# Two attentions of a tuned Trainium2 kernel: scores ahead of the transposes, a division moved, q and k in one bank, one value block moved

## The chip, the cores and the metric

The kernel runs on one core of one Trainium2 chip. The metric is the device time of one execution in microseconds (us), as a median over runs.

A core has five engines that run side by side. Each works through its own instructions strictly in order and waits for others by semaphores. TensorE (PE) does matrix products and transposes into PSUM; its weight loads are listed apart (PEld). VectorE (DVE), ScalarE (ACT) and GpSimd (POOL) do the element work. SyncE (SP) issues the transfers from DRAM.

## The reference, cut to what matters

```python
def layer(i, x):                                   # DEPTH = 2, D = 1024, SEQ = 256, BATCH = 1
    x = post_norm(x, 0.5 * swiglu(x, ffn1_w_in[i], ffn1_w_out[i]))
    x = post_norm(x, fox(x) if i == 0 else mla(x))
    x = post_norm(x, 0.5 * swiglu(x, ffn2_w_in[i], ffn2_w_out[i]))
    return post_norm(x, sigmoid(x @ wg[i] + bg[i]) * (p[i] @ wp[i]))

def fox(x):                                        # layer 0: 16 heads of 64
    q, k, v, f = split(x @ w_in)                   # f: one gate logit per head and token
    cum = cumsum(log_sigmoid(f + b_f), axis=tokens)
    s = q @ k.T / 8 + cum[:, None] - cum[None, :]  # per head, 256 x 256
    return (softmax(causal(s)) @ v) @ w_o

def mla(x):                                        # layer 1: 16 heads, 128 + 64 wide, v 128 wide
    c_q = rms_norm(x @ w_dq)
    q_nope, q_rope = split(c_q @ w_uq); q_rope = rope(q_rope)
    s = (q_nope @ k_nope.T + q_rope @ k_rope.T) / sqrt(192)
    return (softmax(causal(s)) @ v) @ w_o          # k_nope, v from a shared latent c_kv
```

Both attentions sweep blocks of 128 queries. With 256 tokens that is two blocks: the first sees 128 keys, the second 256, so a head's scores fill 128 + 256 = 384 columns of 128 partitions.

## The kernel before

**Precision and weights.** A product in float32 is made of three products of exact parts, high with high, high with low and low with high (`mm3`, whose matmuls are recorded at L418). The parts of a result are made by `parts`: ACT copies the high part (L427), DVE subtracts it to leave the low part (L428). The weights go the same way. A `Stream` knows the order in which weights are used, fetches them into three raw tiles through SP's queue, and splits each unit of up to 1024 columns into a pair: a copy on ACT (L138, about 1.06 us) and a subtraction on DVE (L139, about 1.22 us). Split units wait in ten slots, and in rooms (`ota`, `otb`, `qk`, `fs`) that a stage lends when it doesn't use them. When to split is decided while the program is written: `pump` is called after every `mm3` and issues a split where the next raw tile should have landed and rough clocks of the engines (`busy`, `pair`) say that it holds up nothing. `use` splits at once what is needed now. So moving a step also moves the splits between the steps, on ACT and on DVE.

**What orders the work.** Every engine runs its instructions in the order in which the code issues them. Small steps that should lie between others stand in a queue `bg`: each `use` takes one item off it, and a FoX projection (`ws`) takes one more at its weight blocks 3 and 6. PSUM has three rings of banks of 128 x 512: four `y`, two `h`, two `tr`. Whoever takes a bank waits until its last user but that many is done with it.

**FoX** (function `fox`). The value blocks `V(n, t)` (half n of the columns, tokens t) are projected first: V(0,0), V(1,0), the gates, V(0,1), V(1,1), each into an h bank and then into parts (tag `g`). `gates` puts a chain of eleven items into `bg`: log-sigmoid and running sum of the gate logits on ACT, DVE and POOL (the last of POOL's is L759; ACT's L763 and L764, DVE's L767, L770 and L774 make from it `negc`, the rows that the score product adds). `flush` forces what is left of them, and `gates_transpose` makes `cq`, the per-query terms. Then pairs of heads j = 0 to 7 follow. The steps of a pair:

- `gen_k(j)`, `gen_q(j)`: projections of 24 matmuls each, each into its own h bank and its own parts.
- `QK(j)`: the scores of both heads, two matmuls with `negc` and twelve with q and k.
- `softmax(j)`: four mask steps with a running minimum on DVE (L838), a bias from `cq` (two small operations for each head, L845 and L846), four exponentials on ACT (L850), one reciprocal on DVE (L855), four multiplications by it on POOL (L859). The result is P.
- `T(j)`: six transposes of P into two tr banks (four are recorded at L870, two at L422) and parts PT.
- `AV(j)`: products with the values, into `ota` or `otb`, whose low parts are DVE's L899.
- `O(k, t)`: the output projection of rows k for tokens t.

The loop's order is gen_k(j+1), T(j-1), QK(j), softmax(j), gen_q(j+1), AV(j-1). At j = 7 the projections' places are taken by O(0,0), O(1,0) and O(2,0), O(3,0).

**MLA** (function `mla`). The same steps for one head at a time: `gen(h)` makes k and q in one h bank with one `parts` of 512 columns, `QK(h)` writes into a tr bank, `softmax` has two segments (DVE's mask L1137, ACT's exponentials L1141, reciprocal L1146, POOL's scaling L1148), `T(h)` three transposes, `AV(h)` into an h bank. The order is gen(h+1), T(h-1), QK(h), softmax(h), O(h-2) for both token blocks or, from head `LATE` = 6 on, for the first alone, then a value block V in four of the heads (table `VT`: heads 0, 5, 8 and 10), AV(h-1). The second token block of the late heads follows at the end, partly ahead of the last steps as cover.

Of the kernel before, what the change touches and what calls it, by code (L numbers as in the profile page):

```python
# [13 lines left out]
ALU = mybir.AluOpType  # L14
# [16 lines left out]
LATE = 6  # L31
# [20 lines left out]
class Dummy:  # L52
    """Stands in for engines, pools and tiles while the order of the weights is recorded."""

# [24 lines left out]
class Stream:  # L79
    """Weights in the order of their use: DRAM -> raw tile -> exact pair of float32r parts."""  # L80

# [65 lines left out]
    def lend(self, *tags):  # L147
        """Room that a stage doesn't use."""
        self.retire()
        for t in tags:  # L150
            self.kept.discard(t)
            self.slots.append(t)
# [18 lines left out]
    def busy(self, act=0, dve=0, pe=0):  # L171
        """Keeps rough clocks of the engines, in ns, by the columns that they work on."""
        if act:
            self.act_t = max(self.act_t, self.pe_t) + 200 + 0.84 * act
        if dve:
            self.dve_t = max(self.dve_t, self.pe_t) + 80 + 1.05 * dve
        if pe:
            self.pe_t += max(108, 0.42 * pe)

    def pair(self, n):  # L180
        """The high parts on ScalarE, the low parts on VectorE after them."""
        self.busy(act=n)
        self.dve_t = max(self.dve_t, self.act_t + 100)
        self.busy(dve=n)

    def pump(self):
        """Splits weights ahead of their use where that holds up nothing else."""
        if self.ready == len(self.order) or not self.slots:
            return
        arrival = self.arrives.get(group_of(self.order[self.ready]), 1e12)  # L190
        if arrival <= self.pe_t + 500 and max(self.act_t, self.dve_t) <= self.pe_t + SLACK_NS:
            self.split()
# [29 lines left out]
def unit_of(key, raw):  # L222
    """The part of a raw tile that holds a unit, its partitions and its columns."""
    k, u = key[0], key[-1] % 2
    if k in ("win", "fv"):
        return raw.rearrange("p (k c) -> p k c", c=512)[:, 2 * u : 2 * u + 2, :], 128, 1024
    if k in ("wout", "fo", "pg", "pp", "mo", "qr"):
        return raw[:, 1024 * u : 1024 * u + 1024], 128, 1024
    if k in ("fk", "fq"):
        return raw.rearrange("p (k c) -> p k c", c=256)[:, :, 128 * u : 128 * u + 128], 128, 1024  # L230
    if k == "ff":
        return raw[:, 0:1024], 128, 1024
    if k == "pb":
        return raw[0:1, 0:1024], 1, 1024
    if k == "kd":
        return raw[:, 640 * u : 640 * u + 640], 128, 640
    if k == "dq":
        return raw[:, 768 * u : 768 * u + 768], 128, 768
    if k == "qn":
        return raw[:, 512:1280], 128, 768  # L240
    if k == "kvv":
        return raw[:, 0:1024], 128, 1024
    if k == "kvk":
        return raw[:, 0:512], 128, 512
    raise KeyError(key)
# [83 lines left out]
def pbcast(row, n):  # L329
    """A row of DRAM, read by all partitions."""  # L330
    return bass.AP(tensor=row.tensor, offset=row.offset, ap=[[0, 128], [1, n]])


class Trunk:
# [10 lines left out]
    def own(self, shape, dt, tag):  # L345
        """A tile in room that the weights have given back."""
        self.S.check(tag)
        return self.tl(shape, dt, tag, 1)
# [47 lines left out]
    def spin(self, n):  # L396
        """Keeps the tensor engine's clock up while the first data arrive."""
        hot = self.bank("y")
        for _ in range(n):
            self.nc.tensor.matmul(hot[:, 0:384], self.mask[:, 0:128], self.mask, start=True, stop=True)  # L400
# [7 lines left out]

# [1 line left out]
    def mm3(self, out, lhsT, rhs, start, stop):  # L410
# [14 lines left out]
    def parts(self, hi, lo, src):  # L425
        """src = hi + lo exactly."""
        self.nc.scalar.activation(hi, src, AF.Copy)  # L427
        self.nc.vector.tensor_tensor(lo, src, hi.bitcast(F32), op=ALU.subtract)  # L428
        self.S.pair(cols(src))

    def transposed(self, t, src):
        """Token-major [128, 1024] into xT."""
        for h in range(2):
# [13 lines left out]
    def moving(self, ps, t, name, width, at=None, what=None, sweeps=0):  # L447
        """ps[tokens, width] = x[t] W, the weights moving in units of two k-tiles.

        In sweeps, products of high parts come first, and some low parts come last.  # L450
        """
        order = [(u, terms) for terms in SWEEPS[sweeps] for u in range(4)]
# [22 lines left out]
    def ln_stats(self, st, t, c0, w, y, alpha):  # L475
        """x[t] = alpha x[t] + y in some columns, with their statistics."""
        nc = self.nc
        xs = self.x[t][:, c0 : c0 + w]
        nc.vector.scalar_tensor_tensor(xs, xs, alpha, y, op0=ALU.mult, op1=ALU.add)  # L479
        nc.vector.bn_stats(st, xs)  # L480
        self.S.busy(dve=2 * w)
# [23 lines left out]

# [1 line left out]
    def ffn(self, li, which, lni, kv=False, at=None, cold=False):  # L507
# [81 lines left out]

# [1 line left out]
    def ple_load(self, li):  # L591
# [99 lines left out]

# [1 line left out]
    def fox(self, li):  # L693
# [97 lines left out]
        V(0, 1)  # L791
        V(1, 1)

# [3 lines left out]

        def gen(j, key, c0):
            ps = self.bank("h")
            ws((key, j), ps[:, 0:256])  # L800
            o = qk[:, j % 2]
            self.parts(o[:, 0, c0 : c0 + 256], o[:, 1, c0 : c0 + 256], ps[:, 0:256])

        def gen_k(j):
            gen(j, "fk", 256)

        def gen_q(j):
            gen(j, "fq", 0)

# [19 lines left out]
        def softmax(j):  # L829
# [6 lines left out]
            for s in range(2):  # L836
                for q, (c0, c1) in enumerate(seg):
# [4 lines left out]
                    )  # L842
                c2 = cq[:, 2 * j + s, :]
                i = slice(2 * s, 2 * s + 2)
                nc.vector.tensor_tensor(tt[:, i], nm[:, i], c2, op=ALU.subtract)  # L845
                nc.vector.tensor_tensor(tt[:, i], tt[:, i], c2, op=ALU.add)  # L846
            for s in range(2):
# [6 lines left out]
            self.S.busy(act=1800, dve=1400)  # L854
            nc.vector.reciprocal(su, su)  # L855
            for s in range(2):
                for q, (c0, c1) in enumerate(seg):
                    i = 2 * s + q
                    nc.gpsimd.tensor_scalar(  # L859
                        P[s][:, c0:c1], P[s][:, c0:c1], su[:, i : i + 1], 1.0, op0=ALU.mult, op1=ALU.mult  # L860
                    )
            st[j] = P

        def T(j):
# [42 lines left out]
        def O(k, t):  # L907
# [3 lines left out]
            for n in range(2):  # L911
# [3 lines left out]
                )  # L915

        for j in range(8):
            if j == 2:
# [6 lines left out]
            if j == 0:  # L925
                self.flush()
                gates_transpose()
                S.lend("fs")
            if j >= 1:
                T(j - 1)  # L930
            QK(j, "y" if j < 7 else "h")
            softmax(j)
            if j < 7:
                gen_q(j + 1)
            else:
                O(2, 0)
                O(3, 0)
            if j >= 1:
# [17 lines left out]

# [1 line left out]
    def kv_setup(self):  # L958
# [62 lines left out]

# [1 line left out]
    def mla(self, li):  # L1023
# [106 lines left out]
        def softmax(h):  # L1130
# [14 lines left out]
            self.S.busy(act=900, dve=600)  # L1145
            nc.vector.reciprocal(su[:, 0:2], su[:, 0:2])  # L1146
            for q, (c0, c1) in enumerate(seg):
                nc.gpsimd.tensor_scalar(  # L1148
                    P[:, c0:c1], P[:, c0:c1], su[:, q : q + 1], 1.0, op0=ALU.mult, op1=ALU.mult
                )  # L1150
            st[h] = P

        def T(h):
# [59 lines left out]
        for h in range(16):  # L1213
            if 1 <= h < 15:
                gen(h + 1)
            if h == 15:
                S.lend("qk")
                O(LATE, (1,))
            if h >= 1:
                T(h - 1)  # L1220
            QK(h)
            softmax(h)
            if h >= 2:
                O(h - 2, (0, 1) if h - 2 < LATE else (0,))
            if h == 15:
                O(LATE + 1, (1,))
            if h in VT:
                V(*VT[h], "tr")
            if h >= 1:
                AV(h - 1)  # L1230
        self.load_gb(li, 1)
        O(LATE + 2, (1,))
        O(14, (0,))
        T(15)
        AV(15)
        O(LATE + 3, (1,))
        O(15, (0,))
        self.ln(0, y[0], ALPHA, LN_EPS)
        for h in range(LATE + 4, 16):
            if h == 15:  # L1240
                self.XT(0)
            O(h, (1,))
# [82 lines left out]
```

## Time and profile before

| what | us | share of the span |
|---|---|---|
| median of 3 runs (1127.40, 1127.43, 1129.90) | 1127.43 | |
| span of the profiled execution | 1125.3 | |
| PE busy | 1100.2 | 98% |
| PE weight loads | 922.2 | 82% |
| DVE busy | 715.0 | 64% |
| ACT busy | 543.1 | 48% |
| POOL busy | 79.9 | 7% |

By stage, the windows of the trace give (busy us of each engine in the stretch):

| stretch, us | what runs | length | PE | DVE | ACT | POOL |
|---|---|---|---|---|---|---|
| 0 to 218.8 | first FFN, FoX's V(0,0), V(1,0), gates, V(0,1) | 218.8 | 215.10 | 127.99 | 103.47 | 8.83 |
| 218.8 to 324.8 | FoX, from V(1,1) to AV(7) | 106.0 | 100.34 | 80.93 | 62.76 | 26.18 |
| 324.8 to 768.3 | rest of layer 0, shared keys and values, FFN and MLA's projections | 443.5 | 441.60 | 277.36 | 205.63 | 24.30 |
| 768.3 to 897.7 | MLA's heads | 129.4 | 123.49 | 90.55 | 74.29 | 15.93 |
| 897.7 to 1125.3 | rest of MLA, FFN, end | 227.6 | 219.63 | 138.17 | 97.00 | 4.67 |

How to read rows of the timeline: start, duration, engine, line, operation, output <- input by the program's names, shape, and how many instructions the row groups; in square brackets the idle time before it on that engine and the instruction that ended it. The page gives the profiled execution no time beside its span; the span begins with the first and ends with the last instruction that the profile shows, and the runs' times are 2.1 us longer at the shortest.

### The profile page before, as it was taken

To read this page: it belongs to the slowest core of one execution; us is meant where nothing else is said; L and a number is where in the kernel's file an instruction comes from. 1 tells how busy PE (TensorE), PEld (TensorE's weight loads), DVE (VectorE), ACT (ScalarE), POOL (GpSimd) and SP (SyncE) were. 2 spreads that over 40 slices of the span, in tenths; PEclk is the share of its full clock that TensorE was granted. 3 is DMA by queue.
4 is the path that set the end of the run, shared out by engine and by line. 5 is a ranking of instruction groups with operands and counts; after the bars stand their busy time and mean duration, and the time that the engine had idled before them with its cause. 6 is when DMAs were issued, how large, how long until landed. Compare 5 with 4: busy or idle time off the path is not lost. (4 is left out here: it accounts for less than half of the span.)

```text
span 1125.3 us, 14519 instructions
## 1 busy us (share of the span) xinstructions
PE 1100.2 (98%) x5582; PEld 922.2 (82%) x5582; DVE 715.0 (64%) x1030; ACT 543.1 (48%) x822; POOL 79.9 (7%) x130
## 2 busy tenths in 40 slices
PE   8999999989999999999999999999999999999997
PEld 6888888889878888888888888887899788888886
DVE  5655636777786644557966444488766775554576
ACT  5544533656635544543555444345655454454421
POOL 0000000322210000000320000011111000000000
PEclk9999999989999999999999999999999999999999
DMA  9777644454337765544477665334543566755402
GB/s 298 220 264 249 202 150 131 151 187 151 113 113 225 243 219 183 186 162 148 151 233 243 211 219 166 92 96 140 178 123 113 171 222 221 255 192 182 161 27 75
DMA packets 150537, 198.81 MB, mean 177 GB/s; under 512 B 11714, under 2 KB 128450, under 8 KB 150468
## 3 DMA queue, kind: packets, MB, share of 16 engines
q1 hardware_dynamic: 150468, 197.88, 54.7%
q8 instruction: 44, 0.72, 0.3%
q14 instruction: 25, 0.20, 0.1%
HBM read 196.81 MB, written 1.05 MB: 176 GB/s over the span
## 5 line engine op out<-in xcount | busy, mean ns | idle before, releaser
L139 DVE TENSOR_TENSOR hl<-raw,hl 128x1024 fp32r<-128x1024 f32 (+3 forms) x293 | 345.7, 1197 | 114.9 <-ACT hl L138 109.0
L418 PE MATMUL h<-hl,xT 128*128 128x512 f32 (+1 forms) x1716 | 413.4, 392 | 2.5 <-DVE hl L139 1.5
L418 PEld LDWEIGHTS h<-hl,xT 128*128 128x128 f32 x1716 | 317.4, 188 | 70.4 <-DVE hl L139 2.5
L138 ACT ACTIVATE hl<-raw 128x1024 fp32r<-128x1024 f32 (+3 forms) x293 | 296.0, 1031 | 99.1 <-PE y L418 60.8
L418 PE MATMUL y<-hl,g 128*128 128x512 f32 x792 | 187.1, 391 | 0.0
L418 PEld LDWEIGHTS y<-hl,g 128*128 128x128 f32 x792 | 148.1, 188 | 31.0
L517 ACT ACTIVATE P<-h 128x256 f32<-128x256 f32 x88 | 34.0, 386 | 235.8 <-PE h L418 235.8
L518 DVE TENSOR_TENSOR P<-P,h 128x256 f32<-128x256 f32 x88 | 36.9, 419 | 161.9 <-ACT P L517 161.9
L490 POOL TENSOR_TENSOR rs<-ve,mhalf 128x1 f32<-128x1 f32 x16 | 15.2, 950 | 843.6 <-DVE ve L489 843.6
L427 ACT ACTIVATE xT<-tr 128x512 fp32r<-128x512 f32 x36 | 20.1, 596 | 62.3 <-PE tr L422 62.3
L428 DVE TENSOR_TENSOR g<-tr,g 128x512 fp32r<-128x512 f32 x50 | 34.5, 691 | 24.1 <-ACT g L427 24.0
L418 PE MATMUL h<-xT,hl 128*128 128x256 f32 x360 | 46.8, 289 | 1.8 <-DVE g L428 1.8
L418 PEld LDWEIGHTS h<-xT,hl 128*128 128x128 f32 x360 | 44.8, 197 | 3.1 <-DVE g L428 2.0
L418 PE MATMUL y<-hl,xT 128*128 128x512 f32 (+2 forms) x228 | 44.4, 347 | 0.0
L418 PE MATMUL h<-qk,xT 128*128 128x512 f32 x168 | 43.9, 394 | 0.0
L427 ACT ACTIVATE g<-tr 128x512 fp32r<-128x512 f32 x50 | 29.9, 598 | 24.5 <-PE tr L526 18.6
L418 PEld LDWEIGHTS y<-hl,xT 128*128 128x128 f32 x228 | 37.1, 188 | 5.6 <-issue 0.7
L418 PE MATMUL h<-otb,xT 128*128 128x512 f32 x144 | 37.3, 393 | 0.0
L418 PEld LDWEIGHTS h<-qk,xT 128*128 128x128 f32 x168 | 31.3, 188 | 6.6
L418 PE MATMUL y<-hl,ota 128*128 128x512 f32 x144 | 36.0, 393 | 0.0
L138 ACT ACTIVATE otb<-raw 128x1024 fp32r<-128x1024 f32 x21 | 22.2, 1056 | 20.3 <-PE y L418 14.7
L139 DVE TENSOR_TENSOR qk<-raw,qk 128x1024 fp32r<-128x1024 f32 x21 | 25.8, 1227 | 9.1 <-ACT qk L138 8.8
(204 smaller groups left out, 1289.3 us busy)
## 6 DMA issues: line engine op xcount, KB each, us to landing
raw<-in_ffn_w_in_dram SPq DMA_DIRECT2D x172, 512.0 KB, 5.0
raw<-in_ffn_w_out_dram SPq DMA_DIRECT2D x44, 1024.0 KB, 5.1
raw<-in_fox_w_in_dram SPq DMA_DIRECT2D x12, 1024.0 KB, 5.3
raw<-in_ple_w_gate_dram SPq DMA_DIRECT2D x8, 1024.0 KB, 6.8
raw<-in_mla_w_o_dram SPq DMA_DIRECT2D x8, 1024.0 KB, 6.0
gb<-in_ln_g_dram SPq DMA_DIRECT2D x8, 512.0 KB, 6.9
gb<-in_ln_b_dram SPq DMA_DIRECT2D x8, 512.0 KB, 7.5
raw<-in_fox_w_o_dram SPq DMA_DIRECT2D x4, 1024.0 KB, 5.1
```

The source lines that it names most:

```text
L138: nc.scalar.activation(hi, src, AF.Copy)
L139: nc.vector.tensor_tensor(lo, src, hi.bitcast(F32), op=ALU.subtract)
L418: self.nc.tensor.matmul(out, lhsT, rhs, start=start, stop=stop)
L427: self.nc.scalar.activation(hi, src, AF.Copy)
L428: self.nc.vector.tensor_tensor(lo, src, hi.bitcast(F32), op=ALU.subtract)
L490: nc.gpsimd.tensor_tensor(rs, ve, self.mhalf, op=ALU.pow)
L517: nc.scalar.activation(gt[:, 0:256], ps[:, 0:256], AF.Silu)
L518: nc.vector.tensor_tensor(gt[:, 0:256], gt[:, 0:256], ps[:, 256:512], op=ALU.mult)
```

## The change

Besides docstrings and comments, which are taken out, the change has these parts.

In FoX: (1) V(1,1) is issued inside pair 0, after its softmax and before its division, and no longer ahead of the first key projection. (2) `gen_k` and `gen_q` write into the two halves of one h bank, and one `parts` of 512 columns follows the q projection. (3) The bias is worked out for both heads at once, two operations of 128 x 4 behind all four mask steps. (4) The reciprocal and POOL's scaling become a function `normalize`, which is called after V(1,1) for pair 0, put into the queue `bg` behind one empty item for pairs 1 to 6, and called after O(2,0) for pair 7. (5) QK(j) is issued ahead of T(j-1).

In MLA: QK(h) is issued ahead of T(h-1), the division after the output projection O(h-2), AV(h-1) ahead of the value block V; in head 15 the room `qk` is lent after QK(15), as QK now stands behind O(6, second block). At the end the late second-block projections move one place forward: one stands between T(15) and AV(15), another between AV(15) and O(15, first block).

```diff
-        V(1, 1)
...
-        def gen(j, key, c0):
-            ps = self.bank("h")
-            ws((key, j), ps[:, 0:256])
-            o = qk[:, j % 2]
-            self.parts(o[:, 0, c0 : c0 + 256], o[:, 1, c0 : c0 + 256], ps[:, 0:256])
-        def gen_k(j):
-            gen(j, "fk", 256)
-        def gen_q(j):
-            gen(j, "fq", 0)
+        gen = {}
+        def gen_k(j):
+            gen[j] = self.bank("h")
+            ws(("fk", j), gen[j][:, 256:512])
+        def gen_q(j):
+            ps = gen.pop(j)
+            ws(("fq", j), ps[:, 0:256])
+            o = qk[:, j % 2]
+            self.parts(o[:, 0, :], o[:, 1, :], ps)
...
-                c2 = cq[:, 2 * j + s, :]
-                i = slice(2 * s, 2 * s + 2)
-                nc.vector.tensor_tensor(tt[:, i], nm[:, i], c2, op=ALU.subtract)
-                nc.vector.tensor_tensor(tt[:, i], tt[:, i], c2, op=ALU.add)
+            c2 = cq[:, 2 * j : 2 * j + 2, :].rearrange("p h t -> p (h t)")
+            nc.vector.tensor_tensor(tt, nm, c2, op=ALU.subtract)
+            nc.vector.tensor_tensor(tt, tt, c2, op=ALU.add)
...
+            def normalize():
+                nc.vector.reciprocal(su, su)
+                for s in range(2):
+                    for q, (c0, c1) in enumerate(seg):
+                        i = 2 * s + q
+                        nc.gpsimd.tensor_scalar(
+                            P[s][:, c0:c1], P[s][:, c0:c1], su[:, i : i + 1], 1.0, op0=ALU.mult, op1=ALU.mult
+                        )
...
+        rest = lambda: None
...
+            QK(j, "y" if j < 7 else "h")
             if j >= 1:
                 T(j - 1)
-            QK(j, "y" if j < 7 else "h")
-            softmax(j)
-            if j < 7:
+            normalize = softmax(j)
+            if j == 0:
+                V(1, 1)
+                normalize()
+                gen_q(j + 1)
+            elif j < 7:
+                self.bg.extend((rest, normalize))
                 gen_q(j + 1)
             else:
                 O(2, 0)
+                normalize()
                 O(3, 0)
...
             if h == 15:
+                O(LATE, (1,))
+            QK(h)
+            if h == 15:
                 S.lend("qk")
-                O(LATE, (1,))
             if h >= 1:
                 T(h - 1)
-            QK(h)
-            softmax(h)
+            normalize = softmax(h)
             if h >= 2:
                 O(h - 2, (0, 1) if h - 2 < LATE else (0,))
+            normalize()
             if h == 15:
                 O(LATE + 1, (1,))
+            if h >= 1:
+                AV(h - 1)
             if h in VT:
                 V(*VT[h], "tr")
-            if h >= 1:
-                AV(h - 1)
...
         T(15)
+        O(LATE + 3, (1,))
         AV(15)
-        O(LATE + 3, (1,))
+        O(LATE + 4, (1,))
         O(15, (0,))
         self.ln(0, y[0], ALPHA, LN_EPS)
-        for h in range(LATE + 4, 16):
+        for h in range(LATE + 5, 16):
```

More of the change, by code (lines that the diff above doesn't have):

```diff
@@ L854, in softmax @@
             self.S.busy(act=1800, dve=1400)
[L855 to L861, printed above, removed]
+            def normalize():
[6 more added lines that the diff above has]
+                        )
             st[j] = P
+            return normalize
         def T(j):
@@ L1145, in softmax, with normalize @@
             self.S.busy(act=900, dve=600)
[L1146 to L1150, printed above, removed]
+            def normalize():
+                nc.vector.reciprocal(su[:, 0:2], su[:, 0:2])
+                for q, (c0, c1) in enumerate(seg):
+                    nc.gpsimd.tensor_scalar(
+                        P[:, c0:c1], P[:, c0:c1], su[:, q : q + 1], 1.0, op0=ALU.mult, op1=ALU.mult
+                    )
             st[h] = P
+            return normalize
         def T(h):
```

## The prediction

> **What bounds the kernel now.** I read the page, then the windows by stage, TensorE's timeline through both attentions, and there the queues of VectorE (DVE), ScalarE (ACT) and GpSimd (POOL).
>
> ```profile
> span 1125.3 us, 14519 instructions
> ...
> 218.80:324.80 106.00, 100.34 (x709) 89.18 (x708) 80.93 (x196) 62.76 (x145) 26.18 (x38) 0.97 0.46 146
> ...
> 768.30:897.70 129.40, 123.49 (x818) 110.16 (x817) 90.55 (x191) 74.29 (x160) 15.93 (x34) 1.00 0.44 136
> ```
>
> Columns of a window: length, busy time of PE, weight loads, DVE, ACT, POOL, then granted clock. These are FoX and MLA; PE idles 5.7 and 5.9 us in them. All that the change touches lies here, so it acts only through what PE waits for.
>
> ```profile
> 224.31 2.91 PE L418 MATMUL h<-xT,hl 128*128 128x256 f32 x24
> 229.00 5.90 PE L418 MATMUL h<-xT,hl 128*128 128x256 f32 x48 [1.79 <-DVE g L428]
> 235.05 0.44 PE L418 MATMUL y<-negc,sel 64*128 64x384 f32 x2
> ...
> 244.22 0.78 PE L870 MATMUL tr<-ident,P 128*128 128x128 f32 x2 [2.03 <-POOL P L859]
> 247.21 5.11 PE L418 MATMUL h<-xT,hl 128*128 128x256 f32 x24
> ...
> 264.59 0.60 PE L870 MATMUL tr<-ident,P 128*128 128x128 f32 x4
> ...
> 273.13 0.38 PE L870 MATMUL tr<-ident,P 128*128 128x128 f32 x2
> ```
>
> PE needs 8.54 us for a pair of heads (264.59 to 273.13: two projections of 2.85 us, QK, T, AV). What sets the pace of the later pairs is DVE, which runs this round (pair 3):
>
> ```profile
> 267.70 0.29 DVE L838 CUSTOM_DVE_ANT_0 y<-y,mask 128x128 f32<-128x128 f32 x1
> ...
> 268.80 0.16 DVE L846 TENSOR_TENSOR tt<-tt,cq 128x2 f32<-128x2 f32 x1
> ...
> 269.98 0.16 DVE L846 TENSOR_TENSOR tt<-tt,cq 128x2 f32<-128x2 f32 x1
> 271.26 0.18 DVE L855 RECIPROCAL su<-su 128x4 f32<-128x4 f32 x1 [1.11 <-ACT P L850]
> 272.13 1.29 DVE L139 TENSOR_TENSOR hl<-raw,hl 128x1024 fp32r<-128x1024 f32 x1 [0.70 <-ACT hl L138]
> 273.35 0.41 DVE L428 TENSOR_TENSOR qk<-h,qk 128x256 fp32r<-128x256 f32 x1
> 273.69 0.84 DVE L899 TENSOR_TENSOR ota<-y,ota 64x256 fp32r<-64x256 f32 x2
> 274.56 1.23 DVE L139 TENSOR_TENSOR hl<-raw,hl 128x1024 fp32r<-128x1024 f32 x1
> ...
> 276.16 1.01 DVE L428 TENSOR_TENSOR PT<-tr,PT 128x512 fp32r<-128x512 f32 x2
> 277.09 0.29 DVE L838 CUSTOM_DVE_ANT_0 y<-y,mask 128x128 f32<-128x128 f32 x1
> ```
>
> Mask step to mask step is 9.39 us: 3.56 to the reciprocal, 0.87 to the weight split, 4.96 back to back. DVE idles only where it waits for ACT (1.11 and 0.70). PE's waits for P are what is left over when 9.39 meets 8.54, so covering PE's wait does not shorten the round.
>
> **FoX, the steady round.** Per pair the bias arithmetic goes from four small DVE operations to two (0.2 us each saved), but now stands behind all four mask steps, and all four exponentials of ACT stand behind it.
>
> ```profile
> 269.08 0.37 ACT L850 ACTIVATE P<-y,tt 128x128 f32<-128x128 f32 x1 [2.92 <-DVE tt L846]
> ```
>
> ```profile
> 237.57 1.28 ACT L850 ACT_TABLE_LOAD   x1 [2.24 <-DVE tt L846]
> 238.86 0.37 ACT L850 ACTIVATE P<-y,tt 128x128 f32<-128x128 f32 x1
> ```
>
> ```profile
> 240.62 0.18 DVE L855 RECIPROCAL su<-su 128x4 f32<-128x4 f32 x1 [1.95 <-ACT P L850]
> ```
>
> Before, the first head's exponentials start 1.38 us into the round, under the second head's mask steps. After: both heads' mask steps 1.8, two bias operations 0.36, 0.12 to ACT: start at 2.29; four in a row take 1.76 (238.86 to 240.62); reciprocal at 4.05 instead of 3.56. The "deferred" division does not leave its place: in the built order of pairs 1 to 7 the reciprocal follows the bias operations directly, no split in between. The joined q and k parts are one 128x512 subtraction (0.67 to the next, as PT's first) for two of 0.34: nothing. So 4.05 + 0.87 + 4.96 = 9.88, 0.49 more per pair. QK ahead of T adds PE work of nothing and removes the wait for P; in its place QK's products with the low part of k wait for that joined subtraction, which is queued behind exponentials and a split: 4.05 + 0.87 + 1.22 + 0.69 = 6.83 us into the round. T and PT follow in 0.5 + 1.3 us, just ahead of DVE's own queue (8.9), so 9.88 stands. Pair 1 has three splits in its round instead of two: 11.1.
>
> **FoX, the start.** V(1,1) (24 matmuls, 5.5 us from 218.8 to 224.31; one ACT copy, one DVE subtraction; no DMA, its weights being split for V(0,1)) leaves the place where it covered the gate chain.
>
> ```profile
> 225.84 1.44 POOL L759 TENSOR_SCALAR fs<-fs 32x256 f32<-32x256 f32 x1 [1.08 <-DVE fs L758]
> ```
>
> ```profile
> 227.31 0.30 ACT L763 ACTIVATE negc<-fs 32x128 fp32r<-32x128 f32 x1 [2.21 <-POOL fs L759]
> 227.53 0.40 ACT L764 ACTIVATE negc<-fs 32x256 fp32r<-32x256 f32 x1
> ```
>
> ```profile
> 228.98 0.42 DVE L767 TENSOR_TENSOR negc<-fs,negc 32x256 fp32r<-32x256 f32 x1
> ...
> 230.94 0.35 DVE L774 CAST negc<-negc 64x384 fp32r<-64x384 f32 x1
> ```
>
> POOL's L759 ends at 227.28 in both orders. The changed order then has, on ACT, L763 and L764 (to 227.93) and a split (1.06, to 229.0); on DVE that split's second half (1.22), L767 0.42, L770 0.22, the joined qk 0.67, L774 0.35: QK(0) can start at 231.9. PE has finished V(0,1) at 218.8, three projections of 2.85 and the gate transposes by 227.7: it waits 4.2, where the old wait of 1.79 (for a bank) is gone. Against 235.05 that is 3.1 earlier with 5.5 of V(1,1) still to come.
>
> V(1,1) does cover P(0), so the 2.03 wait goes. What is late next: pair 0's DVE queue. Mask step at 233.3, bias ready 235.5, table load 1.28, exponentials to 238.6; the built order then puts four splits (first ready 239.6, 1.22 each) ahead of V(1,1)'s subtraction: 245.1. gen_k(2) takes the bank that this frees, and PE, done with gen_q(1) at 241.4, waits to 245.1. Then the reciprocal, two splits and qk (248.3), QK(1), T(0) by 249.6, PT, and mask step 1 at 251.2.
>
> ```profile
> 247.31 0.30 DVE L838 CUSTOM_DVE_ANT_0 y<-y,mask 128x128 f32<-128x128 f32 x1 [0.36 <-PE y L418]
> ```
>
> ```profile
> 271.53 2.59 POOL L859 TENSOR_SCALAR P<-P,su 128x128 f32<-128x128 f32 x4 [6.80 <-DVE su L855]
> ```
>
> So +3.9 at mask step 1, +0.1 over pair 1, 5 x 0.49 up to mask step 7, 0.49 to its reciprocal, and 0.5 because T(7), which just met P(7), now waits for POOL's 2.59: **FoX +7.4**. On SP the two 512 KB row loads of pair 2 pass one load of fo, used 20 us later: nothing. Bounds: the start costs 0 if the split is not reached in time on ACT, up to 6 if the T(0) scaling is slow again; the round 0 to 0.8 per pair.
>
> **MLA.** The order becomes gen, QK, T, softmax, O, division, AV.
>
> ```profile
> 782.53 0.78 PE L418 MATMUL h<-PT,g 128*128 128x256 f32 x5 [0.69 <-DVE PT L428]
> ...
> 808.54 0.89 PE L422 MATMUL tr<-ident,P 128*128 128x128 f32 x3 [0.69 <-POOL P L1148]
> ...
> 856.17 0.49 PE L422 MATMUL tr<-ident,P 128*128 128x128 f32 x3
> ...
> 861.75 0.54 PE L422 MATMUL tr<-ident,P 128*128 128x128 f32 x3
> ...
> 880.57 0.73 PE L418 MATMUL y<-hl,fs 128*128 128x512 f32 x2 [0.92 <-ACT fs L427]
> ```
>
> ```profile
> 799.66 0.17 DVE L1146 RECIPROCAL su<-su 128x2 f32<-128x2 f32 x1 [0.70 <-ACT P L1141]
> 800.55 1.27 DVE L139 TENSOR_TENSOR hl<-raw,hl 128x1024 fp32r<-128x1024 f32 x1 [0.72 <-ACT hl L138]
> ```
>
> ```profile
> 799.92 0.82 POOL L1148 TENSOR_SCALAR P<-P,su 128x128 f32<-128x128 f32 x2 [7.38 <-DVE su L1146]
> ```
>
> QK's 1.46 us ahead of T would cover POOL's waits. But here the division does move: in heads 2, 3, 4, 6, 8, 10, 12, 14, 15 the built order has one split before the reciprocal (two in head 3), which costs ACT's 0.9 wait plus 1.2 each. P(h) comes 5.2 us after its mask step instead of 3.0, and the mask step 1.5 after T(h-1): 6.7. T(h) is due 5.58 after T(h-1) in late heads (856.17 to 861.75), 6.95 in those with two O blocks or a V. My walk, place by place: AV(0), which loses QK(1) as cover, +1.0; T(1) -1.5; T(2) +0.2; T(3), behind two splits, +2.3; T(4) -0.7; T(12) +1.25; T(14) +1.2; O(14) -0.2; AV(15), now covered by O(9), -1.25; XT(0), which has one O less over its layer norm, +1.15. **MLA +3.4**; bounds -3 (all waits for P gone, nothing new) and +6 (two splits behind every late head).
>
> **Sum.** 7.4 + 3.4 = 10.8: span 1136.1. The median run is 2.1 above the profiled span, so 1138.
>
> **The rivals.** (a) Slow clock.
>
> ```profile
> 246.50:247.50 1.00, 1.00 (x9) 0.78 (x8) 0.64 (x3) 0.00 (x0) 0.00 (x0) 0.50 1.04 430
> ```
>
> After PE ran no matmul but transposes from 241.7 to 245.3, the clock was 0.50, and 24 matmuls took 5.11 instead of 2.91. If the new wait of 3.7 at gen_k(2) does that, the next projection and QK lose 3: 1141. The same at QK(0) would be hidden, since V(1,1) is ahead of DVE there. For it: one such event. Against: its length is marginal. [...] (b) Faster: DVE's round closes under PE's 8.54. Then the 0.85 per pair that PE loses now (five pairs, 4.2), the wait of 2.0 and the slow stretch (3.0) go, less 2.4 more at QK(0): 1120. For it: DVE is busy 80.93 of 106; against: its round would have to shrink by 1.3. It decides from 8.54 per pair. (c) FoX as told, MLA's division is early enough and only waits go (-3): 1132. (d) Gains and losses cancel, or the reorder is absorbed: 1127.
>
> **How the numbers follow.** The forecast as told gets 0.54, because each of its terms is read from a queue in the built order; its own range, 1133 to 1143, is the sum with the round's cost at 0.2 to 0.7 per pair and the start's at 2 to 5. Rival (a) gets 0.10, (b) 0.14, (c) 0.12, (d) 0.10. To hold eight in ten the range goes from just under (d) to past (a): 1126 to 1144, which leaves out (b) and the tails. A change of 0.3% (3.4 us) is about what a measurement of this kernel can tell from none: faster is (b) alone, 0.14; within it (d), 0.10; slower the other three, 0.76.
>
> **What would show it.** Right: a PE wait of about 4 us at the first negc matmul, one near 4 at gen_k(2) released by DVE g; in pairs 2 to 6 PE idle ended by DVE qk instead of POOL P; DVE's mask steps 9.9 apart, its wait at the reciprocal 1.9 instead of 1.11; MLA waits at T(3), T(12), T(14). Wrong: mask steps 8.6 to 9.4 apart, or QK(0) unheld.

## The result, and the profile after

The changed kernel takes 1142.33 us (median of 4 runs, 1139.96 to 1144.14), the kernel before 1128.08 beside it: a ratio of 1.0127, 95% interval 1.0113 to 1.0141. It is slower, as forecast (1138, range 1126 to 1144), and the loss is larger than forecast. The profiled execution is the one of 1139.96 us. Of all the executions in this document one was slow, 3889.86 us among the twelve of the last version tried, and the ratios leave it out.

From its page, the span and the busy time of each engine:

```profile
span 1137.7 us, 14483 instructions
...
PE 1100.9 (97%) x5582; PEld 921.2 (81%) x5582; DVE 711.8 (63%) x1006; ACT 541.3 (48%) x814; POOL 83.7 (7%) x130
```

PE does the same work (1100.9 us, 1100.2 before) in 12.4 us more of span. So 11.7 of the 12.4 us are PE waiting. Of the engines that do the element work only POOL has become busier, by 3.8 us, with the same 130 instructions.

The windows by stage, from the same PE instruction to the same as before (FoX, then MLA; the columns are those of the prediction):

```profile
218.80:330.30 111.50, 99.29 (x710) 87.56 (x709) 77.36 (x172) 60.25 (x137) 24.94 (x38) 0.98 0.42 138
773.80:910.10 136.30, 124.74 (x817) 110.43 (x816) 90.91 (x191) 74.86 (x160) 22.10 (x34) 1.00 0.44 137
```

FoX grew from 106.0 to 111.5 and MLA from 129.4 to 136.3. By PE's landmarks, the same PE instructions in both traces, that is 5.5 and 7.0, together the whole 12.4; the stretches between and behind are equal to 0.1 us. POOL's busy time in MLA went from 15.93 to 22.10.

What PE waited for in FoX, before (first fence) and after; the columns are total us, times, longest:

```profile
PE tr L870 <- POOL P L859: 3.2, 5, 2.0
PE h L418 <- DVE g L428: 1.8, 1, 1.8
```

```profile
PE y L418 <- DVE qk L428: 4.8, 5, 1.0
PE y L418 <- DVE negc L774: 3.8, 1, 3.8
PE h L418 <- DVE g L428: 1.4, 1, 1.4
PE h L418 <- DVE qk L428: 1.1, 1, 1.1
PE y L418 <- ACT qk L427: 0.9, 1, 0.9
```

The waits of the transposes for P are gone, as the change intends. In their place the scores wait for q and k, once for the gate chain (`negc`), and a projection waits for V(1,1)'s bank (`g`). The row of 1.1 us is QK(7), which waits for an h bank.

The same view of MLA, before (first fence) and after:

```profile
PE tr L422 <- POOL P L1148: 1.7, 2, 1.1
```

```profile
PE tr L422 <- POOL P L1159: 6.1, 8, 1.2
PE tr L422 <- DVE x L495: 1.4, 2, 0.9
PE h L418 <- DVE PT L428: 1.3, 1, 1.3
```

Here the transposes wait for P more than before: 6.1 us in eight waits, where before there were two, of 1.05 us at T(1) and 0.69 at T(4).

The start of FoX on PE:

```profile
231.18 0.44 PE L418 MATMUL y<-negc,sel 64*128 64x384 f32 x2 [3.78 <-DVE negc L774]
231.43 0.88 PE L418 MATMUL y<-qk 64*128 64x128 f32 x12
232.24 7.35 PE L418 MATMUL h<-hl,xT 128*128 128x512 f32 x24
...
243.74 3.01 PE L418 MATMUL h<-xT,hl 128*128 128x256 f32 x24 [1.41 <-DVE g L428]
```

And the clock in two windows of it, in V(1,1) (first line) and during the wait for `negc` ahead of it:

```profile
232.80:235.40 2.60, 2.60 (x8) 2.03 (x7) 1.47 (x8) 0.95 (x1) 0.00 (x0) 0.50 0.70 182
227.40:231.10 3.70, 0.00 (x0) 0.00 (x0) 2.94 (x6) 2.00 (x3) 0.00 (x0) 1.00 0.31 111
```

PE idles 3.78 us, does 14 small matmuls, and V(1,1) then runs partly at a clock of 0.50: 7.35 us where it took 5.5.

DVE's steady round in FoX (pair 3, as in the prediction):

```profile
270.64 0.29 DVE L837 CUSTOM_DVE_ANT_0 y<-y,mask 128x128 f32<-128x128 f32 x1
...
272.32 0.16 DVE L843 TENSOR_TENSOR tt<-nm,cq 128x4 f32<-128x4 f32 x1
272.52 0.16 DVE L844 TENSOR_TENSOR tt<-tt,cq 128x4 f32<-128x4 f32 x1
274.59 0.18 DVE L855 RECIPROCAL su<-su 128x4 f32<-128x4 f32 x1 [1.92 <-ACT P L848]
275.47 1.36 DVE L139 TENSOR_TENSOR hl<-raw,hl 128x1024 fp32r<-128x1024 f32 x1 [0.70 <-ACT hl L138]
276.76 0.68 DVE L428 TENSOR_TENSOR qk<-h,qk 128x512 fp32r<-128x512 f32 x1
...
280.47 0.29 DVE L837 CUSTOM_DVE_ANT_0 y<-y,mask 128x128 f32<-128x128 f32 x1
```

Mask step to mask step is 9.83 us (9.39 before); DVE's wait at the reciprocal is 1.92 instead of 1.11.

Head 3 of MLA, on DVE, POOL and PE:

```profile
805.98 2.36 DVE L139 TENSOR_TENSOR hl<-raw,hl 128x1024 fp32r<-128x1024 f32 x2 [1.58 <-ACT hl L138]
808.26 0.16 DVE L1157 RECIPROCAL su<-su 128x2 f32<-128x2 f32 x1
808.33 0.41 DVE L428 TENSOR_TENSOR ota<-h,ota 128x256 fp32r<-128x256 f32 x1
808.65 1.64 DVE L139 TENSOR_TENSOR hl<-raw,hl 128x512 fp32r<-128x512 f32 x2
```

```profile
808.61 2.03 POOL L1159 TENSOR_SCALAR P<-P,su 128x128 f32<-128x128 f32 x2 [7.23 <-DVE su L1157]
```

```profile
809.54 0.33 PE L422 MATMUL tr<-ident,P 128*128 128x128 f32 x1 [1.04 <-POOL P L1159]
810.70 0.44 PE L422 MATMUL tr<-ident,P 128*128 128x128 f32 x2 [0.82 <-POOL P L1159]
```

The reciprocal stands behind two splits, and then the two scalings take 2.03 us; before, they took 0.82 or 0.83 in every head but one (1.26). That second part was not in the prediction.

### The profile page after: what moved, and what is told of

Its sections match the earlier page's. It is cut to its first block, busy times and chain, and to the rows that moved or that the text cites. A ratio compares the mean times of both kernels' runs of the same rounds, so it can differ in the third digit from the quotient of the medians.

```text
span 1137.7 us, 14483 instructions
## 1 busy us (share of the span) xinstructions
PE 1100.9 (97%) x5582; PEld 921.2 (81%) x5582; DVE 711.8 (63%) x1006; ACT 541.3 (48%) x814; POOL 83.7 (7%) x130
## 3 DMA queue, kind: packets, MB, share of 16 engines
HBM read 196.81 MB, written 1.05 MB: 174 GB/s over the span
## 4 chain that ended last, share of the span: by engine, by line
PE 78%; DVE 10%; ACT 5%; issue 3%; POOL 2%; DMA 1%; SPq 0%; DVEq 0%; ACTq 0%; POOLq 0%
PE h L418 47%; PE y L418 27%; DVE hl L139 3%; ACT hl L138 2%; PE tr L526 2%; PE tr L422 2%; PE tr L418 1%; ACT P L848 1%; DVE PT L428 1%; POOL P L1159 1%; ACT P L1150 1%; DVE y L837 1%; DVE qk L428 1%; DVE x L495 1%; ACT PT L427 1%
## 5 line engine op out<-in xcount | busy, mean ns | idle before, releaser
L418 PE MATMUL h<-hl,xT 128*128 128x512 f32 x1728 | 418.5, 393 | 2.0 <-DVE hl L139 1.5
L418 PEld LDWEIGHTS h<-hl,xT 128*128 128x128 f32 x1728 | 320.9, 189 | 70.9 <-DVE hl L139 2.6
L428 DVE TENSOR_TENSOR g<-tr,g 128x512 fp32r<-128x512 f32 x50 | 34.6, 691 | 25.2 <-ACT g L427 25.2
L418 PE MATMUL h<-xT,hl 128*128 128x256 f32 x360 | 44.1, 280 | 1.4 <-DVE g L428 1.4
L418 PEld LDWEIGHTS h<-xT,hl 128*128 128x128 f32 x360 | 42.5, 188 | 1.8 <-DVE g L428 1.6
L418 PEld LDWEIGHTS h<-otb,xT 128*128 128x128 f32 x144 | 26.8, 188 | 5.7
L428 DVE TENSOR_TENSOR xT<-tr,xT 128x512 fp32r<-128x512 f32 x36 | 23.3, 683 | 13.0 <-ACT xT L427 13.0
```

The lines of the kernel that those rows point to most:

```text
L418: self.nc.tensor.matmul(out, lhsT, rhs, start=start, stop=stop)
```

## The experiments

All ratios are to the kernel before, run beside it (medians 1128.3 to 1128.8). A stretch at half clock costs PE some 2 to 3 us (24 matmuls took 5.11 us instead of 2.91 in the kernel before, AV(0) to T(1) 6.80 instead of 3.85 in the run with the early division), and where such a stretch lay differed from trace to trace (244 to 252 us in the kernel before, 232 to 236 in the changed one, by windows of 2 us); so mechanisms are read from waits, rounds and landmarks rather than from a few us of time.

**Each attention alone.** FoX changed, MLA as before:

> The changed kernel with the MLA function of before; FoX keeps all its changes. Theory (the two attentions lose separately, 5.45 us in FoX and 6.96 in MLA by TensorE's landmarks in the two traces): a span near 1130.7, time near 1133 to 1135, about 0.6% above before, and MLA's waits of TensorE as before (1.7 us for GpSimd's P). Rival (MLA's loss comes with FoX, by weights or a clock that the shift upsets): the time stays near 1142, or falls to 1128.

Measured: 1136.35 us, ratio 1.0065 (1.0040 to 1.0090), 1.4 us above the theory's range. MLA changed, FoX as before:

> The changed kernel with the FoX function of before; MLA keeps all its changes. Theory (separate losses): span near 1132.3, time near 1134.5, about 0.6% above before; TensorE's waits for GpSimd's P in MLA stay at 6.1 us. Rival (the parts only lose together): below 1130.

Measured: 1133.76 us, ratio 1.0047 (1.0030 to 1.0065), span 1132.2, waits for P in MLA 5.8 us. The two lose separately; the shares of 0.65% and 0.47% add up to 1.12% of the 1.27%. FoX has the larger share in the times, MLA in the landmarks. Part of that may be the clock: the trace of FoX alone has MLA, which is unchanged in it, at 130.9 us for 128.3, with a half-clock stretch from 889 to 896. The other executions have no trace.

**MLA's division, early again.**

```diff
-            normalize = softmax(h)
+            softmax(h)()
             if h >= 2:
                 O(h - 2, (0, 1) if h - 2 < LATE else (0,))
-            normalize()
```

> The changed kernel, but in MLA the division (reciprocal and scaling) is issued right after the exponentials again, ahead of O(h-2); QK ahead of T, AV ahead of V and the tail stay as changed. The order of the splits is the same, only the reciprocal moves ahead of one or two of them. Theory (the place of the division makes MLA's loss, by lateness and by scaling that runs beside DVE's splits): GpSimd's scaling goes back to 0.82 us for two in every head, TensorE's waits for P fall from 6.1 us to under 1, span near 1131.5, time near 1136. Rival (the loss is made by QK's, AV's and the tail's new places): span stays at 1137 to 1138.

Measured: 1135.24 us, ratio 1.0059 (1.0041 to 1.0078), span 1133.3. No wait of PE for P is left in MLA. The scaling of head 3, and a window of the clock:

```profile
808.48 0.83 POOL L1159 TENSOR_SCALAR P<-P,su 128x128 f32<-128x128 f32 x2 [7.45 <-DVE su L1157]
```

```profile
788.60:796.00 7.40, 6.64 (x31) 6.64 (x32) 4.20 (x11) 3.15 (x8) 0.83 (x2) 0.54 0.33 89
```

MLA took 130.6 us from its first transposes to XT(0) instead of 135.2. This trace has a slow stretch in MLA which the changed kernel's has not: from AV(0) to T(1) it took 6.80 instead of 3.85. Less those 2.95, MLA would be at 127.6, where the kernel before has 128.3. The times say the same: with the division early the whole changed kernel takes 1135.24 us, and 1136.35 with the whole of MLA as before. So the place of the division makes MLA's loss, and QK's, AV's and the tail's new places together cost nothing that these runs can tell (the intervals are 2 to 3 us to each side).

**Late or held up?** The scaling moved to DVE, at the same late place:

```diff
-                    nc.gpsimd.tensor_scalar(
+                    nc.vector.tensor_scalar(
                         P[:, c0:c1], P[:, c0:c1], su[:, q : q + 1], 1.0, op0=ALU.mult, op1=ALU.mult
                     )
```

> The changed kernel, but MLA's scaling by the reciprocal runs on DVE, right behind the reciprocal, in the same late place; no GpSimd scaling is left in MLA. Theory (in heads 2, 3, 4 and 6 GpSimd's scaling is held up by DVE's splits beside it, 1.9 to 2.3 us instead of 0.82): without it P is ready about 0.6 us after the reciprocal, waits for P at T(2), T(4), T(6) vanish, T(3)'s falls from 1.9 to about 0.5, those of T(12) and T(14), whose scaling took 0.82, stay near 0.8 to 1.0 each: 2.4 instead of 6.1 us, span near 1134. Rival (only the late reciprocal matters, the engine of the scaling doesn't): waits of 5 us or more, span 1137.

Measured: 1138.65 us, ratio 1.0097 (1.0073 to 1.0121); MLA 131.9 instead of 135.2 by landmarks, waits for P 3.2 instead of 6.1 us. T(2)'s and T(6)'s waits are gone, T(3)'s is still 1.69:

```profile
809.70 0.55 DVE L1159 TENSOR_SCALAR P<-P,su 128x128 f32<-128x128 f32 x2
```

```profile
810.13 0.61 PE L422 MATMUL tr<-ident,P 128*128 128x128 f32 x3 [1.69 <-DVE P L1159]
```

So about half of the waits came from lateness (T(3), T(12) and T(14)) and half from the long scaling. T(3)'s expected 0.5 was wrong: two splits ahead of the reciprocal suffice for nearly the whole wait of 1.86.

**What makes the scaling long.** The kernel before, with one idle DVE operation per MLA head:

```diff
             nc.vector.reciprocal(su[:, 0:2], su[:, 0:2])
+            nc.vector.tensor_tensor(qn, self.mask, self.mask, op=ALU.subtract)
```

> The kernel of before with one more DVE operation in each MLA head, directly behind the reciprocal: a subtraction of 128x384 with both inputs in SBUF whose result nobody uses; it falls into the 0.72 us in which DVE waits for ACT. Theory (a DVE operation with two SBUF inputs holds up GpSimd's scaling): the two scalings of a head take about 1.2 to 1.4 us instead of 0.82. Rival (they run side by side, and the long scalings have another cause): 0.82 as before.

Measured: 1130.77 us in its one run. DVE and POOL in head 3:

```profile
799.27 0.17 DVE L1146 RECIPROCAL su<-su 128x2 f32<-128x2 f32 x1 [0.70 <-ACT P L1141]
799.35 0.54 DVE L1147 TENSOR_TENSOR nrm<-mask 128x384 f32<-128x384 f32 x1
800.15 1.23 DVE L139 TENSOR_TENSOR hl<-raw,hl 128x1024 fp32r<-128x1024 f32 x1 [0.26 <-ACT hl L138]
```

```profile
799.53 2.11 POOL L1149 TENSOR_SCALAR P<-P,su 128x128 f32<-128x128 f32 x2 [6.04 <-DVE su L1146]
```

The two scalings take 1.05 us in the six heads where no split follows at once, 1.56 and 1.57 in the two (1 and 10) where one of 512 columns does, and 2.10 to 2.18 in the eight with one of 1024; PE's waits for P rise from 1.7 to 6.4 us. The hold-up is confirmed and is larger than expected. In head 3 the second scaling alone is this row:

```profile
800.11 1.53 POOL L1149 TENSOR_SCALAR P<-P,su 128x256 f32<-128x256 f32 x1
```

It begins as the split begins (800.15) and ends 0.26 us after the split's end (801.38). The first (799.53, 0.60 us) ends 0.24 us after the end of the 0.54 us subtraction (799.89). So in these rows each scaling lasts until just after the whole DVE operation beside it. Before, the first 0.72 us behind the reciprocal were free on DVE (it waited for ACT's copy, and the split began at 800.55), and both of POOL's scalings began in that gap:

```profile
800.27 0.48 POOL L1148 TENSOR_SCALAR P<-P,su 128x256 f32<-128x256 f32 x1
```

A busy DVE alone does not do it. In the changed kernel's heads 8, 10, 12 and 14 the operations beside the scaling are subtractions with one input in PSUM (L428) instead of splits, and the scaling takes 0.82 or 0.83 us. In head 12:

```profile
873.31 0.82 POOL L1159 TENSOR_SCALAR P<-P,su 128x128 f32<-128x128 f32 x2 [7.08 <-DVE su L1157]
```

```profile
873.36 0.68 DVE L428 TENSOR_TENSOR qk<-h,qk 128x512 fp32r<-128x512 f32 x1
```

So what holds the scaling up, as far as these runs show, are DVE operations with both inputs in SBUF: two scalings take 0.82 us in a gap of 0.72 between them, 1.05 behind one of 0.54, 2.11 with a split of 1.23 as well. By what means they do it no run shows.

**FoX's bias, per head again.**

```diff
+                c2 = cq[:, 2 * j + s, :]
+                i = slice(2 * s, 2 * s + 2)
+                nc.vector.tensor_tensor(tt[:, i], nm[:, i], c2, op=ALU.subtract)
+                nc.vector.tensor_tensor(tt[:, i], tt[:, i], c2, op=ALU.add)
-            c2 = cq[:, 2 * j : 2 * j + 2, :].rearrange("p h t -> p (h t)")
-            nc.vector.tensor_tensor(tt, nm, c2, op=ALU.subtract)
-            nc.vector.tensor_tensor(tt, tt, c2, op=ALU.add)
```

> The changed kernel, but in FoX the bias is worked out per head again, two operations of 128x2 behind each head's two mask steps. Theory (DVE's round sets FoX's pace, and the joined bias makes the exponentials late): mask step to mask step in pairs 3 to 6 falls from 9.8 to about 9.4, six rounds, span near 1135. Rival (the round is set by the joined q and k parts that QK waits for): the round stays at 9.8 and the span at 1137.7.

Measured: 1139.44 us, ratio 1.0092 (1.0069 to 1.0115), span 1135.1. The six rounds from mask step 1 fall from 60.27 to 58.29 us together; single ones reach 9.39 and 9.25, the two before them only 9.83 and 9.62, in which this trace has a half-clock stretch (266 to 272). FoX ends 2.5 us earlier. The joined operations, two fewer per pair, cost more than they save, because they stand between the first head's mask steps and its exponentials.

**V(1,1) back at its old place**, ahead of gen_k(0):

> The changed kernel, but V(1,1) is issued ahead of gen_k(0) again, and pair 0 divides right after its exponentials. Theory (the start of FoX loses because V(1,1)'s place opens a wait for the gate chain and puts V(1,1)'s subtraction behind four splits): the 3.8 us wait at QK(0) and the wait at gen_k(2) for V(1,1)'s parts go, V(1,1) runs at full clock, mask step 1 comes near 246 instead of 250.0, span near 1134. Rival (the start was bound by DVE's splits, wherever V(1,1) stands): mask step 1 stays at 249 to 250 and the span at 1137.

Measured: 1137.80 us, ratio 1.0080 (1.0065 to 1.0095), span 1134.7. QK(0) no longer waits for `negc`, V(1,1) runs at full clock (1.00 from 218 to 224), mask step 1 is at 247.5 instead of 250.0 and FoX ends 3.1 us earlier. Not as good as expected at mask step 1: QK(1) now waits 1.9 and 1.2 us for its own q and k parts.

**q and k in banks and parts of their own again:**

> The changed kernel, but q and k have their own h banks and their own parts again. Theory (covering or moving TensorE's wait does not shorten DVE's round): the wait for q and k parts shrinks and turns up elsewhere, the round stays within 0.15 of 9.83, span 1137 to 1138.5. Rival (the joined subtraction behind the exponentials sets the pace): the waits of about 1 us at QK go, the round falls to 9.0 or less, span near 1132.

Measured: 1141.34 us, ratio 1.0116 (1.0099 to 1.0133), span 1140.1. From pair 2 on the round does not shorten (9.7 to 10.7). It was to stay within 0.15 of 9.83, and two rounds are longer than that, both at a half-clock stretch (268 to 276); the span is 1.6 us above the theory's range. The waits for q and k parts shrink, and waits for the banks of value blocks take their place (4.3 us in two, the longest 3.3). So taking the shared bank and the joined parts back wins nothing that the times can tell (1141.34 against 1142.33).

**Is DVE's round the pace?** A split taken out of the round's busy part and put where DVE waits, first in the kernel before, behind the bias in pairs 1 to 6:

```diff
+            if 1 <= j <= 6 and not self.rec:
+                S.retire()
+                if S.slots and group_of(S.order[S.ready]) in S.raw:
+                    S.split()
```

> The kernel of before; in FoX pairs 1 to 6 the split that followed the reciprocal is issued between the bias and the exponentials, so that ACT copies under the mask steps and DVE subtracts while it waited for the exponentials (1.11 us) and for ACT's copy (0.70). Theory (DVE's round of 9.39 sets FoX's pace, and its two waits are in it): the round falls to between 8.5 and 8.8, TensorE's waits at T for GpSimd's P nearly go after pair 1, span 1121 to 1122. Rival (the round is set by the chain from mask step to P and T, in which the exponentials now come later): 9.4 or more, span 1125 or above.

Measured: 1123.47 us, ratio 0.9954 (0.9937 to 0.9971), span 1123.6: 0.5% faster than before, and 1.6 us above the theory's range. DVE in pairs 3 and 4:

```profile
270.85 1.22 DVE L139 TENSOR_TENSOR hl<-raw,hl 128x1024 fp32r<-128x1024 f32 x1
272.05 0.18 DVE L859 RECIPROCAL su<-su 128x4 f32<-128x4 f32 x1
...
277.04 0.29 DVE L838 CUSTOM_DVE_ANT_0 y<-y,mask 128x128 f32<-128x128 f32 x1
...
285.58 0.29 DVE L838 CUSTOM_DVE_ANT_0 y<-y,mask 128x128 f32<-128x128 f32 x1
```

The waits for the exponentials and for ACT's copy are filled, and the round is 8.54 us: what PE needs. The move also takes the split away from beside POOL's scaling, which falls from 2.59 to 1.63 us. The round of before did not hang on that, as DVE went from its weight split to the next mask step without a wait. The same four lines in the changed kernel:

> The changed kernel, with the split of pairs 1 to 6 that follows the reciprocal issued between the bias and the exponentials (as was done to the kernel of before). Theory (DVE's round of 9.83 is the pace of the changed FoX, and 1.8 us of waiting for exponentials and 0.77 for ACT's copy are in it): the round falls to between 8.5 and 8.8, TensorE's waits for the joined q and k parts nearly go, span near 1132. Rival (the joined parts behind the exponentials bound QK): 9.4 or more, span 1136 or above.

Measured: 1132.77 us, ratio 1.0040 (1.0026 to 1.0054), span 1130.3. The rounds from pair 2 on are 8.3 to 8.8, and of the waits for q and k only 0.2 us is left in FoX. Both orders of QK and T were paced by DVE.

**A version that beats both.** The kernel before with that split, and QK ahead of T only where T had to wait:

```diff
+            if j == 1:
+                QK(j, "y")
             if j >= 1:
                 T(j - 1)
-            QK(j, "y" if j < 7 else "h")
+            if j != 1:
+                QK(j, "y" if j < 7 else "h")
...
+            if h in (2, 5):
+                QK(h)
             if h >= 1:
                 T(h - 1)
-            QK(h)
+            if h not in (2, 5):
+                QK(h)
```

> The kernel of before with the split between bias and exponentials, and QK ahead of T only where T waited for P: pair 1 in FoX, heads 2 and 5 in MLA. Theory: T(0)'s wait of 2.0 falls to about 1 and the slow clock after it shrinks, T(1)'s 1.05 and T(4)'s 0.69 go; 3 to 5 us below the version with the split alone: 1118 to 1121. Rival (QK waits for its own parts there, or the next mask step comes no earlier): 1122 to 1124.

Measured: 1121.83 us, ratio 0.9940 (0.9927 to 0.9953): between the two expectations, 0.8 above the theory's range and 0.2 below the rival's. The gain over the split alone is 1.6 us by the medians, and the intervals overlap; by the traces FoX ends 3.8 us earlier. Pair 1's round falls from 11.07 to 8.65; QK(1) waits 0.6 and 0.9 us for its parts. In MLA the waits of T(1) and T(4) are gone, and one of 0.70 at T(2) is new. One step more, q and k of a pair in one bank, with parts of their own:

> The same with q and k of a pair in one h bank, but each with its own parts as in before. Theory: gen_q(0) no longer waits 1.8 us for V(1,1)'s bank, and QK(0) comes up to 1.8 us earlier, for which the gate chain is ready; 1 to 2 us below the version with two banks. Rival (DVE's queue behind QK(0) sets mask step 1 anyway): no difference.

Measured: 1128.54 us (the others of the twelve 1124.74 to 1129.17), ratio 0.9994 (0.9981 to 1.0007). The step lost what the others had gained:

```profile
232.09 7.76 PE L418 MATMUL h<-xT,hl 128*128 128x256 f32 x48 [4.58 <-DVE qk L428]
```

gen_q(0) writes into the bank that k's parts are read from, and waits for that subtraction, which stands behind the gate chain on DVE. Neither theory had this wait.

## Why the prediction was right, and by how much each step was off

The forecast, slower by 10.8 us of span in two separate attentions, held; the span grew by 12.4. That the sum came so near is partly luck: FoX was over-sized by 1.9 us and MLA under-sized by 3.6. The terms one by one:

| step of the prediction | forecast | measured |
|---|---|---|
| QK(0) starts, held by the gate chain | 231.9, wait 4.2 | 231.18, wait 3.78 |
| gen_k(2) waits for V(1,1)'s bank | 3.7 | 1.41 |
| mask step 1 | 251.2 (+3.9) | 250.00 (+2.7) |
| pair 1's round | 11.1 | 10.81 |
| later rounds | 9.88 | 9.72 to 9.84, the last 10.24 |
| FoX in all | +7.4 | +5.5 |
| AV(0) without QK(1) as cover | +1.0 | +1.1 |
| T(1) | -1.5 | -1.6 |
| T(2) | +0.2 | +1.5 |
| T(3), behind two splits | +2.3 | +2.0 |
| T(4) | -0.7 | -0.1 |
| T(6) | 0 | +1.0 |
| T(12), T(14) | +2.45 | +2.9 |
| O(14) | -0.2 | -0.2 |
| AV(15), then XT(0) | -1.25, +1.15 | -1.05, +1.4 |
| MLA in all | +3.4 | +7.0 |

**FoX, the start, was over-sized by 1.2 us at mask step 1,** and 1.0 of it comes from one reading: "POOL's L759 ends at 227.28 in both orders". It ended at 226.24:

```profile
225.83 0.41 POOL L759 TENSOR_SCALAR fs<-fs 32x256 f32<-32x256 f32 x1 [1.09 <-DVE fs L758]
```

Before, it took 1.44 us, and these splits ran beside it on DVE:

```profile
225.78 2.56 DVE L139 TENSOR_TENSOR hl<-raw,hl 128x1024 fp32r<-128x1024 f32 x2
```

With V(1,1) gone from there DVE was idle beside L759, and the operation took 0.41 us. POOL's busy time from 216 to 230 us is 4.53 to 4.56 us in all seven traces in which V(1,1) has its new place, and 5.56 to 5.60 in all seven in which it has its old one: the same 1.03. So the gate chain came 1.0 us earlier than told, pair 0's mask step at 232.32 instead of 233.3, and V(1,1)'s parts freed their bank at 243.7 instead of 245.1. PE came to that bank 0.9 us later than told, because its clock fell in V(1,1), which took 7.35 us instead of 5.5. That is why gen_k(2) waited 1.41 instead of 3.7. The prediction had said of a slow stretch at this place that it would be hidden behind DVE, and it was. Where V(1,1) ran at full clock in the changed order (separate banks, clock 1.00 from 232 to 238, 5.79 us), the wait was 3.26.

**FoX, the round, was right in mechanism and size:** 9.83 for 9.88. It is shown by both sides: the per-head bias shortens it, a split moved into the wait brings it to 8.54, and changing the banks does not shorten it. (8.54 is the kernel before with that split; the changed kernel with it has 8.3 to 8.8.) "Covering PE's wait does not shorten the round" stands.

**T(7) was to come another 1.0 later than mask step 7, and came 0.1 later:** mask step 7 is 5.3 behind before, T(7)'s last transposes 5.4. The prediction priced the scaling there with the 2.59 of pair 3. That of pair 7 is short in both kernels, before (first fence) and after:

```profile
308.79 1.63 POOL L859 TENSOR_SCALAR P<-P,su 128x128 f32<-128x128 f32 x4 [6.46 <-DVE su L855]
```

```profile
314.58 1.62 POOL L859 TENSOR_SCALAR P<-P,su 128x128 f32<-128x128 f32 x4 [7.66 <-DVE su L855]
```

With the 1.2 of mask step 1 and 0.3 of pair 1 this makes FoX's error, less 0.4 for rounds that grew a little more than told.

**MLA was under-sized by half,** and the term that failed is "P(h) comes 5.2 us after its mask step". It priced the late division by the splits ahead of the reciprocal and took POOL's scaling at the 0.82 of the kernel before. That 0.82 was itself a product of the place: it fell into DVE's wait for ACT. Beside DVE's splits it takes 1.9 to 2.3 in heads 2, 3, 4 and 6, where P(h) came 6.4 to 7.7 us after its mask step, and that is the error at T(2), T(4) and T(6). In heads 8, 12 and 14, without splits beside the scaling, P(h) came after 5.3 to 5.6 us, nearly as told. (Before, P(h) took 3.2 us, not the 3.0 of the prediction.) The two experiments with the scaling on DVE and with the idle subtraction show it. The page of before had shown the same in FoX, where four scalings took 2.59; the prediction used that row and did not ask why. So L759, T(7) and MLA have one error in common: a duration on POOL was carried to a place where DVE does other work beside it.

**The rest of the distance to the median,** 1142.33 against the profiled 1139.96, goes with the clock: the records give TensorE 0.997 of full speed in the profiled execution and 0.991 to 0.993 in the other three. Runs of the kernel before show the same, 1124.66 us at 0.999 and 1129.64 at 0.990. So the median lies nearer to rival (a), 1141, than to the forecast of 1138, but that rival's mechanism is not shown: in the profiled execution the slow stretch came at QK(0) instead of gen_k(2) and was hidden, and where it came in the other three no trace tells. The rival of MLA's waits only going (-3) is refuted; so is the faster one, since the round went away from 8.54. Its threshold was right: brought to 8.54 by other means, the kernel is faster than before.

What stays open: why slow stretches come at different places in traces of kernels with equal work there (behind equal waits at QK(0), 3.80 and 3.78 us, the clock from 230 to 232 was 0.53 with FoX alone and 1.00 in the changed kernel), and how the loss divides exactly between V(1,1)'s place (3.1) and the bias (2.5), each taken back alone; their sum of 5.6 fits the 5.5 only if they don't overlap.

## What to carry to other kernels

Find the engine whose round sets the pace, list the gaps in that round with what ends each, and fill them with its own work (9.39 us became 8.54 here); reordering another engine to cover its wait left the round as it was (9.7 to 10.7 us with separate banks, 9.83 without). When a step moves to a new place on one queue, price its followers anew: a duration measured in a gap (0.82 us) need not hold beside another engine's work (2.03 beside splits). A small saving of instructions can lengthen a round if it moves the start of what everyone waits for behind them (six rounds took 60.27 us with the joined bias, 58.29 without).

## What the runs showed that was not expected

- GpSimd's scalings lasted until 0.24 to 0.26 us after the DVE operations with two SBUF inputs beside them (head 3 with the idle subtraction): two scalings took 0.82 us alone or beside DVE operations that read PSUM, 1.05 behind one short subtraction of 0.54, 2.11 with a split of 1.23 as well.
- Two halves of one PSUM bank did not decouple PE and its reader: the q projection waited 4.58 us for the subtraction that read the k half.
- With waits of 3.26 to 4.58 us TensorE's clock fell to 0.50 for about 3 to 7 us by windows of 2 us, in the last part of the wait or behind it: at QK(0) in the six traces with a wait of 3.78 to 3.80, at gen_k(2) with separate banks (3.26), at gen_q(0) with one bank (4.58). In other traces such stretches followed shorter waits (2.03 at T(0) in the kernel before; 1.92 and 1.16 at QK(1) with V(1,1) back) with transposes and a few small matmuls between them. What sets the clock back is not shown.
